# Splitting the mixers' weight chunks in one piece of 1024 columns instead of two of 512, all but the first

## The chip, the cores and the metric

The kernel runs on one core of a Trainium2 chip. The metric is the time of one execution on the device in microseconds (us): the median of the runs of the kernel before is 599.97 us (3 runs, 599.6 to 600.78). The profile is of one execution of its own.

## What is computed

The reference is a small decoder of two layers for 256 tokens of width 1024 in float32. Each layer has a mixer (self-attention and attention to a fixed memory, then an output projection) and an MLP with a squared ReLU of width 4096. Cut to what matters:

```python
# layer A
h = _rmsnorm(x, a_norm_attn);  z = h @ a_w_in          # q, k, v, qm
o_self = _diff_attention(rope(q), rope(k), v, lam, lam_init, a_subln)
o_mem = _memory_attention(qm, mem, a_mem_norm, a_w_mem_kv)
x = x + concat([o_self, o_mem]) @ a_w_out
x = x + relu(_rmsnorm(x, a_norm_mlp) @ a_w_up)**2 @ a_w_down
# layer B
k, v = _rmsnorm(x, kv_norm) @ w_kv;  z = _rmsnorm(x, b_norm_attn) @ b_w_in
o_self = _moba_attention(rope(q), rope(k), v)          # one block: causal attention
o_mem = _memory_attention(qm, mem, b_mem_norm, b_w_mem_kv)
x = x + concat([o_self, o_mem]) @ b_w_out
x = x + relu(_rmsnorm(x, b_norm_mlp) @ b_w_up)**2 @ b_w_down
return _rmsnorm(x, final_norm)
```

## The kernel before

**Weights.** All weights lie in DRAM as 192 chunks of 128 x 1024 float32 (512 KB each). `chunk()` (line 319) loads one into a buffer `w`, makes its high part `wh` with a cast on ACT (line 336) and its low part `wl` = w - wh with a subtraction on VectorE (DVE, line 338). Every matrix product then takes three matmuls on TensorE (PE): h·wh, h·wl, l·wh, where h and l are the high and low part of the activations. `split_scaled` (line 351) makes those, with one ACT instruction (L352) and one DVE instruction (L354) for a tile of 128 x 256.

The split of a chunk is done in two halves of 512 columns or in one piece, by `st_["pieces"]`. It starts at 2, `mlp_up` (line 778) sets it to 1 for a layer's MLP, and the end of `mlp` (line 996) sets it back to 2. So the 64 chunks of the two mixers are split in halves, those of the MLPs in one piece. A matmul that uses columns of one half waits for the split of that half alone.

**Stages.** A mixer has 24 chunks for its projections (`nat_block`, line 484, matmuls of 128 x 512 at L499; K tile k uses half k % 2 of chunk k // 2) and 8 for the output projection (`out_proj`, line 754). There, chunk after chunk, 8 blocks of three matmuls of 128 x 256 (L765) use one tile of 128 rows of the attention's output. The tiles are taken in the order of `OUT`: 4, 5, 6, 7, 0, 1, 2, 3. A tile comes from `finish_o` (line 628): two PE transposes of one pair of heads (L634), then L352 and L354. In layer A the attention's output is scaled before that: L721 (PE), L725 and L732 (ACT), a row of small DVE instructions ending with L399, and L744 on POOL. L586 (scores), L624 and L681 are other matmuls and transposes of the attention. The MLPs (L821 up, L871 down) follow each mixer.

**Order.** Every piece of work is a step of a planner (class `Plan`, line 59). Steps are added in program order; a step's priority is its number in that order, less a shift for its kind from the table `EARLY` (line 31), unless `pri` gives a number by hand; the lower goes first. `Plan.order` (line 118) plays the steps on the engines with a duration set for each, takes for a free engine the ready step of the best priority, and so fixes the order in which each engine's instructions are emitted. Each engine then runs its own in that order, one behind the other. Buffers are counted: 4 of class `w`, 6 of `wh`, 6 of `wl` (line 233). A chunk gets a buffer when a chunk before it has been used up, and `w`, `wh` and `wl` are given out in program order.

**The start.** A loop at the end of the kernel (lines 1274 to 1283) adds the loads of x in two parts (`xa` with the first four tiles of 256 tokens, `xb` with the last four, priority 3), the first four chunks, and the splits of x's eight tiles. The first chunk is loaded in two halves. Line 1282 sets by hand the priority of the step that stands fifth from the end of the list of steps, just after a chunk has been added: with one DMA step and four split steps that is the chunk's DMA. All loads are issued by SyncE (SP).

Of the kernel before, what the change touches and what calls it, by code (L numbers as in the profile page):

```python
# [208 lines left out]
def t_act(n, psum=False, scale=False):  # L209
    return (51 if psum else 93) + 0.835 * n + (93 if scale else 0)  # L210


def t_dve(n, scalar=False):
    return 69 + 1.041 * n + (61 if scalar else 0)
# [11 lines left out]
def tile_hybrid(ctx: ExitStack, tc: tile.TileContext, xa, xb, memt, xnat, mnat, w0, wall, consts, fgain, out):  # L226
# [17 lines left out]
    def buf(cls, shape, dt=F32, pool=None):  # L244
        pool = pool or ring
        return Buf(cls, lambda slot: pool.tile(shape, dt, name=name(cls), tag=f"{cls}{slot}", bufs=1))

    def bank(cls):
        return buf(cls, [128, 512], F32, psum)
# [62 lines left out]
    def dma(dst, src, nbytes, r=(), w=(), pri=None):  # L312
        P.add(("dma", max(470, nbytes / (290 if nbytes <= 2100 * 128 else 390)), lambda: nc.sync.dma_start(dst(), src)),
              r, w, lag=1900, pri=pri)


    st_ = {"i": 0, "pieces": 2, "layer": "A"}

    def chunk(dma_pieces=1):
        i = st_["i"]  # L320
        st_["i"] += 1
        w = buf("w", [128, CW])
        h = buf("wh", [128, CW], F32R)
        l = buf("wl", [128, CW], F32R)
        hs = (0, 1)
        if dma_pieces == 1:
            dma(lambda: w.t, wall[i], 4 * 128 * CW, w=[(w, 0), (w, 1)])
        else:
            for p in hs:
                dma(lambda p=p: w.t[:, p * 512:(p + 1) * 512], w0[p], 256 * CW, w=[(w, p)], pri=2 * p - 1.5)  # L330
        old, P.shift = P.shift, EARLY["w" + st_["layer"]]
        for p in (hs if st_["pieces"] == 2 else [hs]):
            q = p if isinstance(p, tuple) else (p,)
            sl = slice(q[0] * 512, q[-1] * 512 + 512)
            n = 512 * len(q)
            P.add(("act", t_act(n), lambda sl=sl: nc.scalar.copy(h.t[:, sl], w.t[:, sl])),  # L336
                  [(w, x) for x in q], [(h, x) for x in q])
            P.add(("dve", t_dve(n), lambda sl=sl: nc.vector.tensor_sub(l.t[:, sl], w.t[:, sl],  # L338
                                                                       h.t[:, sl].bitcast(F32))),
                  [(w, x) for x in q] + [(h, x) for x in q], [(l, x) for x in q], port=True)  # L340
        P.shift = old
        return h, l
# [8 lines left out]
    def split_scaled(src, skey, gain, T, k, psrc=False):  # L351
        P.add(("act", t_act(S, psrc, True), lambda: nc.scalar.activation(T.h(k), src(), AF.Copy, scale=gain)),  # L352
              skey, [T.hk(k)])
        P.add(("dve", t_dve(S, True), lambda: nc.vector.scalar_tensor_tensor(  # L354
            T.l(k), src(), gain, T.h(k).bitcast(F32), op0=OP.mult, op1=OP.subtract)),
            list(skey) + [T.hk(k)], [T.lk(k)], port=not psrc)
# [393 lines left out]
    def add_x(m, ps, off):  # L750
        P.add(("dve", t_dve(S), lambda: nc.vector.tensor_add(xT[:, m], xT[:, m], ps.t[:, off:off + S])),  # L751
              [ps, ("x", m)], [("x", m)])
# [59 lines left out]
    def ukeys(us, k):  # L812
        return [(us[k // 4], k // 2), (us[k // 4], k // 2, 1)]
# [21 lines left out]
    def block_sums():  # L835

        sums = {}
        for i, j in enumerate(FAST):
            if i < 2:
                b = ppx_buf()  # L840
                dst, keys = (lambda b=b: b.t), [b]
            elif i < 5:
                dst = lambda i=i: vb.rearrange("p a b e -> p (a b e)")[:, (i - 2) * 512:(i - 1) * 512]
                keys = [("vb", n, hf) for n in range(2) for hf in range(2)]
            else:
                dst, keys = (lambda: mv.rearrange("p a b e -> p (a b e)")), [("mv", 0), ("mv", 1)]
            sums[j] = dst, keys + [("s", j)]
        st_["sums"] = sums
        return sums
# [102 lines left out]
    def mlp(st, done):  # L952
        us = mlp_up(st, block_sums())
        pss = {(hf, c): bank("t") for c in range(2) for hf in range(2)}
        ys = {(hf, c): buf("q" + "hl"[c], [128, 512]) for hf, c in pss}

        def gather(more):
            r1, r5, r6, r7 = more

            def add(y, x, r):  # L960
                y, x = ys[y], ys[x]
                P.add(("dve", t_dve(512), lambda: nc.vector.tensor_add(y.t, x.t, r.t)), [x, r] + [y] * (x is y), [y])
            P.add(("act", t_act(512, True), lambda: nc.scalar.copy(ys[0, 0].t, r1.t)), [r1], [ys[0, 0]])
            add((0, 1), (0, 0), r6)
            add((1, 0), (0, 1), r7)
            add((1, 1), (1, 0), r5)
            add((0, 1), (0, 1), r5)

        part = 24
        _, product, u_ = natural_down(us, pss, part, part, gather,  # L970
                                      wsum, lambda a: [("wsum", a)], 4)
        for c in range(2):
            for k in range(part, 32):
                i = k % 2
                if i == 0:
                    ch = chunk()
                for hf in range(2):
                    product(pss[hf, c], u_(k, hf), lambda ch=ch, i=i: [b.t[:, i * 512:i * 512 + 512] for b in ch], 0, 512,
                            k == 31, ukeys(us, k) + [(b, i) for b in ch])
            for hf in range(2):  # L980
                y, ps = ys[hf, c], pss[hf, c]
                P.add(("dve", t_dve(512), lambda y=y, ps=ps: nc.vector.tensor_add(y.t, y.t, ps.t)), [y, ps], [y])
            for b in range(2):
                ps = bank("t")

                def turn(c=c, b=b, ps=ps):
                    for i in range(2):
                        for hf in range(2):
                            o = b * 256 + i * 128
                            nc.tensor.transpose(ps.t[:, i * S + hf * 128:i * S + hf * 128 + 128],  # L990
                                                ys[hf, c].t[:, o:o + 128], ident)
                P.add(("pe", 4 * 110 + 85, turn), [ys[0, c], ys[1, c]], [ps])
                for i in range(2):
                    add_x(4 * c + 2 * b + i, ps, i * S)
                    done(4 * c + 2 * b + i)
        st_["pieces"] = 2

    def mlp_last(st):

# [275 lines left out]
    for k in range(KT):  # L1275
        if k == 0:
            dma(lambda: xg[:, 0:NG + 4 * S], xa, 512 * (NG + 4 * S), w=["g"] + [("x", j) for j in range(4)], pri=-1)
        if k == 4:
            dma(lambda: xg[:, NG + 4 * S:], xb, 512 * 4 * S, w=[("x", j) for j in range(4, 8)], pri=3)
        if k % 2 == 0:  # L1280
            first_ch.append(chunk(2 if k == 0 else 1))
            P.steps[-5].pri = k - 0.5 if k else P.steps[-5].pri
        split_scaled(lambda k=k: xT[:, k], [("x", k), "g"], g["a_norm_attn"][:, k:k + 1], xn, k)
# [27 lines left out]
    rx = Stats()  # L1311
    xq = big_tiles(2, 3)
    mlp(ma, x_prep("kv_norm", xn, rx))

    def mem_b():
# [86 lines left out]
```

## Time and profile before

| | |
|---|---|
| median of 3 runs | 599.97 us (599.6 to 600.78) |
| span of the profiled execution | 725.8 us |
| mean granted TensorE clock in it | 0.755 |
| PE busy | 716.6 us, 99% of the span |
| DVE busy | 491.3 us, 68% |
| ACT busy | 398.0 us, 55% |
| DMA, mean rate | 149 GB/s |

The page gives no time of the profiled execution beside its span, which is 126 us longer than the median of the runs. How to read the lines that follow: a group is line, engine, operation, tile written <- tiles read, shape, then busy time in us, mean duration in ns, and after the second bar the idle time of the engine just ahead of these instructions with what ended it. A row of the timeline is start, length, engine, line, operation, tiles and count (neighbours of a kind stand in one row), with the idle time before it in brackets. A row of the chain of work that ended last is start, length, engine and line.

### The profile page before, as it was taken

How to read it: one execution, taken by the hardware profiler on the slowest of the kernel's cores; microseconds unless marked ns; L12 is line 12 of the kernel's file. 1: busy time of each engine (PE TensorE's matmuls, PEld its weight loads, DVE VectorE, ACT ScalarE, POOL GpSimd, SP SyncE). 2: the span in 40 equal slices, each digit the busy share in tenths (PEclk: the TensorE clock that was granted, in tenths of full speed). 3: DMA queues.
4: the chain of work that ended last, by engine and by line, in shares of the span. 5: the costliest groups of instructions: out<-in, count | busy, mean ns of one | idle time of the engine just before them, and what ended most of it. 6: DMA issues, size and time to landing. Idle time of an engine off the chain costs nothing.

```text
span 725.8 us, 10368 instructions
## 1 busy us (share of the span) xinstructions
PE 716.6 (99%) x3794; PEld 590.5 (81%) x3794; DVE 491.3 (68%) x871; ACT 398.0 (55%) x750; POOL 54.4 (8%) x67
## 2 busy tenths in 40 slices
PE   9999999999999999999999999999999999999996
PEld 7676769999999977677777776889999999776775
DVE  5777666587556687766776577675675666876664
ACT  6776666455544554444575477656464455554422
POOL 0121110030000000000111121001200000000002
PEclk8777777777777777777777777777777777777777
DMA  8854432435444433546455432224444443354421
GB/s 303 293 183 165 146 95 79 145 119 175 151 168 146 152 139 132 188 145 209 139 174 179 169 120 85 88 88 143 153 164 152 154 158 125 127 186 151 148 85 59
DMA packets 30003, 108.45 MB, mean 149 GB/s; under 512 B 3328, under 2 KB 3328, under 8 KB 29696
## 3 DMA queue, kind: packets, MB, share of 16 engines
q1 hardware_dynamic: 29664, 107.26, 43.4%
q8 instruction: 30, 0.49, 0.3%
q10 hardware_dynamic: 288, 0.52, 0.2%
q14 instruction: 21, 0.17, 0.1%
HBM read 106.72 MB, written 1.05 MB: 148 GB/s over the span
## 4 chain that ended last, share of the span: by engine, by line
PE 98%; DVE 1%; DMA 1%; ACT 0%; issue 0%; SPq 0%; ACTq 0%
PE acc L821 30%; PE acc L499 23%; PE t L871 23%; PE acc L765 7%; PE acc L871 6%; PE t L586 2%; PE t L624 2%; PE t L681 1%; PE t L557 1%; DMA xT<-xa 1%; PE t L1013 0%; PE t L990 0%; DVE xT L751 0%; PE t L579 0%; PE t L721 0%; PE t L720 0%
## 5 line engine op out<-in xcount | busy, mean ns | idle before, releaser
L336 ACT CAST wh<-w 128x512 fp32r<-128x512 f32 (+1 forms) x232 | 182.5, 814 | 191.3 <-PE acc L821 74.0
L338 DVE TENSOR_TENSOR wl<-w,wh 128x512 fp32r<-128x512 f32 (+1 forms) x232 | 213.4, 939 | 86.7 <-ACT wh L336 71.7
L821 PE MATMUL acc<-xn,wh 128*128 128x256 f32 x1024 | 157.3, 314 | 0.5 <-DVE xn L354 0.5
L821 PEld LDWEIGHTS acc<-xn,wh 128*128 128x128 f32 x1024 | 150.7, 224 | 0.7 <-DVE xn L354 0.7
L871 PE MATMUL t<-wh,B 128*128 128x512 f32 (+1 forms) x368 | 134.4, 453 | 0.0
L499 PE MATMUL acc<-wh,xn 128*128 128x512 f32 x256 | 101.6, 472 | 0.7 <-ACT xn L352 0.7
L871 PEld LDWEIGHTS t<-wh,B 128*128 128x128 f32 x368 | 72.5, 199 | 29.8
L821 PE MATMUL acc<-xn,wl 128*128 128x256 f32 x512 | 84.1, 314 | 0.0
L871 PE MATMUL t<-wl,B 128*128 128x512 f32 (+1 forms) x184 | 82.9, 450 | 0.0
L821 PEld LDWEIGHTS acc<-xn,wl 128*128 128x128 f32 x512 | 78.1, 224 | 0.0
L499 PEld LDWEIGHTS acc<-wh,xn 128*128 128x128 f32 x256 | 51.0, 199 | 23.5 <-issue 2.2
L765 PE MATMUL acc<-B,wh 128*128 128x256 f32 x256 | 60.1, 323 | 0.0
L499 PE MATMUL acc<-wl,xn 128*128 128x512 f32 x128 | 58.0, 453 | 0.0
L790 DVE SCALAR_TENSOR_TENSOR u<-acc,rb 128x512 f32<-128x512 f32 x32 | 21.9, 690 | 50.5 <-PE acc L821 50.5
L871 PEld LDWEIGHTS t<-wl,B 128*128 128x128 f32 x184 | 37.0, 201 | 15.1
L765 PEld LDWEIGHTS acc<-B,wh 128*128 128x128 f32 x256 | 46.3, 216 | 0.9 <-issue 0.8
L452 POOL TENSOR_TENSOR sqa<-sqa,sq 128x256 f32<-128x256 f32 x21 | 20.3, 966 | 295.7 <-ACT sq L451 294.9
L765 PE MATMUL acc<-B,wl 128*128 128x256 f32 x128 | 40.0, 313 | 0.0
L895 DVE TENSOR_TENSOR wl<-wsum,wh 128x1024 fp32r<-128x1024 f32 x24 | 29.4, 1223 | 8.9 <-ACT wh L894 6.5
L533 POOL TENSOR_TENSOR ropet<-ropes,consts 128x256 f32<-128x256 f32 (+1 forms) x28 | 25.1, 917 | 129.0 <-ACT ropes L522 106.5
L499 PEld LDWEIGHTS acc<-wl,xn 128*128 128x128 f32 x128 | 26.8, 210 | 9.1
L894 ACT CAST wh<-wsum 128x1024 fp32r<-128x1024 f32 x24 | 25.3, 1052 | 15.9 <-PE acc L871 6.9
(223 smaller groups left out, 899.1 us busy)
## 6 DMA issues: line engine op xcount, KB each, us to landing
w<-wall SPq DMA_DIRECT2D x191, 512.0 KB, 3.3
w<-memt SPq DMA_DIRECT2D x4, 512.0 KB, 5.0
B<-xnat SPq DMA_DIRECT2D x1, 1024.0 KB, 7.4
B<-mnat SPq DMA_DIRECT2D x1, 1024.0 KB, 8.9
xT<-xa SPq DMA_DIRECT2D x1, 540.0 KB, 3.8
w<-w SPq DMA_DIRECT2D x2, 256.0 KB, 3.5
xT<-xb SPq DMA_DIRECT2D x1, 512.0 KB, 6.6
consts<-consts SPq DMA_DIRECT2D x1, 256.5 KB, 4.5
```

What stands on the lines that cost most here:

```text
L336: P.add(("act", t_act(n), lambda sl=sl: nc.scalar.copy(h.t[:, sl], w.t[:, sl])), [(w, x) for x in q], [(h, x) for x in q])
L338: P.add(("dve", t_dve(n), lambda sl=sl: nc.vector.tensor_sub(l.t[:, sl], w.t[:, sl], h.t[:, sl].bitcast(F32))), [(w, x) for x in q] + [(h, ...
L452: P.add(("pool", t_pool(S), lambda: nc.gpsimd.tensor_tensor(self.acc.t, self.acc.t, sq.t, op=OP.add)), [sq, self.acc], [self.acc])
L499: nc.tensor.matmul(pss[hf].t[:, c0:c1], a(k)[:, ts], b.t[:, o + c0:o + c1], start=(k == 0 and i == 0), stop=(k == KT - 1 and i == 2))
L533: nc.gpsimd.tensor_tensor(t.t[:, 0:nh, e:e + 32], zs.t[:, 0:nh, 32 - e:64 - e], b(sin[:, e:e + 32]), op=OP.mult)
L586: nc.tensor.matmul(sp[hd].t[:, c], qk[a].t[r, qb * 128:(qb + 1) * 128], qk[b].t[r, S:S + c.stop - c.start], start=(qb == 0 and i == 0 and ...
L765: nc.tensor.matmul(o, a.t[:, ws], x(k), start=(n == 0 and m % 2 == 0 and i == 0), stop=(n == KT - 1 and i == 2), skip_group_check=True)
L790: P.add(("dve", t_dve(512, True), lambda u=u, ps=ps: nc.vector.scalar_tensor_tensor(u.t, ps.t.rearrange("p (a s) -> p a s", a=2), 0.0, rb_ ...
L821: nc.tensor.matmul(ps.t[:, o], w.t[:, k * 128:(k + 1) * 128], xnt[:, k, x], skip_group_check=True, **flags)
L871: nc.tensor.matmul(ps.t[:, c0:c1], x, y, start=start and i == 0, stop=stop and i == 2, skip_group_check=True)
L894: P.add(("act", t_act(m), lambda: nc.scalar.copy(h[x].t[:, :m], src())), keys, [h[x]])
L895: P.add(("dve", t_dve(m), lambda: nc.vector.tensor_sub(l[x].t[:, :m], src(), h[x].t[:, :m].bitcast(F32))), keys + [h[x]], [l[x]], port=True)
```

## The change

`mlp` no longer sets `st_["pieces"]` back to 2, and the loop of the start sets it to 2 for the first chunk and to 1 for the others. With that, 63 of the 64 mixer chunks are split by one ACT and one DVE instruction of 128 x 1024.

```diff
@@ mlp
                 for i in range(2):
                     add_x(4 * c + 2 * b + i, ps, i * S)
                     done(4 * c + 2 * b + i)
-        st_["pieces"] = 2
@@ the start
         if k % 2 == 0:
+            st_["pieces"] = 2 if k == 0 else 1
             first_ch.append(chunk(2 if k == 0 else 1))
             P.steps[-5].pri = k - 0.5 if k else P.steps[-5].pri
```

A chunk that is split in one piece adds three steps to the planner's list, not five. The step that is fifth from the end in line 1282 is then no longer the chunk's DMA, but a split step of a tile of x that was added before it; the DMAs of chunks 1, 2 and 3 keep the priority of their place in the list. And as every mixer chunk adds two steps fewer, the numbers from which priorities are made are others, so that the planner puts the steps of both mixers in another order, on all engines. The order of the MLPs is nearly the same.

At the start of SP's queue (w_224 is the first chunk, w_230 or w_234 the second, xT<-xa and xT<-xb the halves of x; - is before, + is after):

```order
 L313 DMA xT_66<-xa 128x1080
 L313 DMA w_224<-w 128x512
-L313 DMA w_230<-wall 128x1024
 L313 DMA xT_66<-xb 128x1024
-L313 DMA w_246<-wall 128x1024
-L313 DMA w_261<-wall 128x1024
+L313 DMA w_234<-wall 128x1024
+L313 DMA w_242<-wall 128x1024
+L313 DMA w_257<-wall 128x1024
 L313 DMA consts_68<-consts 128x513
```

The second half of x has moved ahead of the second chunk. At the same place on ACT (xn are the split tiles of x, w_230 and w_234 the second chunk):

```order
 L352 ACTIVATE xn_67<-xT_66 128x256 x3
 L336 CAST wh_228<-w_224 128x512
-L352 ACTIVATE xn_67<-xT_66 128x256
-L336 CAST wh_254<-w_230 128x512 x2
+L352 ACTIVATE xn_67<-xT_66 128x256 x5
+L336 CAST wh_270<-w_234 128x1024
```

All splits of x's tiles now stand ahead of the second chunk's cast. At the end of layer A's mixer, on ACT before (t_1484 and t_1505 are the transposes of the last two pairs of heads, B_275_1058 the high parts of the attention's output):

```order
L725 ACTIVATE o_1420<-t_1405,rs_175 128x128 x2
L732 ACTIVATE dg_1431,msq_180<-o_1420 128x128 x2
L336 CAST wh_1466<-w_1223 128x1024
L352 ACTIVATE B_275_1058<-t_1484,consts_68 128x256
L336 CAST wh_1503<-w_1304 128x1024
L352 ACTIVATE B_275_1058<-t_1505,consts_68 128x256
```

and in the changed kernel (t_1462 and t_1468 are the same two transposes, wh_1434 and wh_1457 chunks of the MLP):

```order
L725 ACTIVATE o_1402<-t_1392,rs_175 128x128 x2
L732 ACTIVATE dg_1413,msq_180<-o_1402 128x128 x2
L336 CAST wh_1434<-w_1198 128x1024
L336 CAST wh_1457<-w_1271 128x1024
L352 ACTIVATE B_276_1014<-t_1462,consts_68 128x256
L352 ACTIVATE B_276_1014<-t_1468,consts_68 128x256
```

Both casts now stand ahead of both L352; on DVE the subtractions of the same chunks stand ahead of both L354 likewise. On PE at the same place, in the changed kernel (wh_1128 is chunk 5 and wh_1169 chunk 6 of the output projection, acc are its sums):

```order
L765 MATMUL acc_1157<-B_276_1014,wh_1128 128x256
L765 MATMUL acc_1157<-B_276_1014,wl_1145 128x256
L765 MATMUL acc_1157<-B_278_1021,wh_1128 128x256
L634 MATMUL t_1462<-ident_122,o_1330 128x128 x2
L634 MATMUL t_1468<-ident_122,o_1402 128x128 x2
L765 MATMUL acc_1130<-B_276_1014,wh_1169 128x256
L765 MATMUL acc_1130<-B_276_1014,wl_1183 128x256
L765 MATMUL acc_1130<-B_278_1021,wh_1169 128x256
```

The transposes of both pairs stand between chunk 5's last matmul and chunk 6's first. Before, 30 matmuls of chunks 4 and 5 stood between the first of them and chunk 6, and 18 between the second and chunk 6.

## The prediction

> **What bounds the kernel now.** I read the page first: the span, the busy shares, the granted clock and the shares of the chain of work that ended last.
>
> ```profile
> span 725.8 us, 10368 instructions
> PE 716.6 (99%) x3794; PEld 590.5 (81%) x3794; DVE 491.3 (68%) x871; ACT 398.0 (55%) x750; POOL 54.4 (8%) x67
> PEclk8777777777777777777777777777777777777777
> PE 98%; DVE 1%; DMA 1%; ACT 0%; issue 0%; SPq 0%; ACTq 0%
> core 0: 725.8 us, clock 0.755
> ```
>
> The last row is from the view of the cores. In this execution TensorE (PE) is busy for 716.6 of 725.8 us and the chain is PE for 98%. Two engines feed it: ACT makes the high part of each weight chunk, VectorE (DVE) the low part. They have 45% and 32% of idle time, so shorter splits by themselves buy nothing here. But the granted clock is 0.755, and the span stands 126 us above the median of the runs, 599.97. The timed runs therefore had another balance, which bounds as follows. PE work at full clock would be about 716.6 x 0.75 = 537 us. With the 9 us in which PE is not busy that makes 546, so the 600 leave some 54 us for waits if the clock was full; without any further wait, 600 - 9 = 591 us for the same work means a clock of 537 / 591 = 0.91. The truth lies between: a clock of 0.91 and no waits, or full clock and 54 us of waits for ACT, DVE or DMA. I look for where such waits would be, in the windows by stage (columns: window, its length, busy time of PE, PEld, DVE, ACT and POOL with counts, granted clock, DMA share, GB/s).
>
> ```profile
> 10.00:50.00 40.00, 40.00 (x161) 28.06 (x159) 28.47 (x61) 28.12 (x65) 6.49 (x6) 0.75 0.76 267
> 50.00:100.00 50.00, 50.00 (x226) 35.83 (x223) 37.39 (x94) 35.90 (x109) 6.92 (x8) 0.75 0.41 133
> 100.00:150.00 50.00, 49.51 (x327) 44.17 (x326) 31.76 (x77) 31.79 (x84) 3.85 (x6) 0.75 0.33 108
> 400.00:450.00 50.00, 50.00 (x234) 35.16 (x233) 32.49 (x66) 31.68 (x79) 10.34 (x12) 0.75 0.36 119
> 450.00:500.00 50.00, 50.00 (x349) 43.19 (x348) 30.77 (x73) 27.85 (x71) 0.00 (x0) 0.75 0.30 99
> ```
>
> At full clock PE would need 30 us for the first row and 37.5 for the second; DVE is busy for 28.5 and 37.4 there. So layer A's mixer is where DVE would bind in a faster run, and the mixers are what the change touches.
>
> **What the larger pieces save.** The groups with their shapes kept apart:
>
> ```profile
> L338 DVE TENSOR_TENSOR wl<-w,wh 128x1024 fp32r<-128x1024 f32 x104 | 127.7, 1229 | 51.0 <-ACT wh L336 37.0 <-PE acc L821 9.8 <-PE acc L871 2.1
> L336 ACT CAST wh<-w 128x1024 fp32r<-128x1024 f32 x104 | 109.1, 1051 | 151.5 <-PE acc L821 74.0 <-PE t L871 61.3 <-PE acc L765 14.7
> L338 DVE TENSOR_TENSOR wl<-w,wh 128x512 fp32r<-128x512 f32 x128 | 85.8, 704 | 35.6 <-ACT wh L336 34.7 <-issue 0.8
> L336 ACT CAST wh<-w 128x512 fp32r<-128x512 f32 x128 | 73.4, 621 | 39.8 <-PE acc L499 24.6 <-PE t L871 5.7 <-DMA w<-wall 3.6
> ```
>
> 128 halves are the 64 mixer chunks. 63 of them become one piece: 63 instructions fewer on ACT and 63 on DVE. Twice a mean is too much, since neighbours overlap: two halves in a row take 1.14 us on ACT and 1.29 on DVE (rows below), so a chunk saves about 0.09 on ACT and 0.06 on DVE, together 63 x 0.09 = 5.7 us and 63 x 0.06 = 3.8 us. In the profiled execution this is beside a busy PE: worth 0. In a timed run it is worth at most the 3.8 us of the tighter engine. I take 0.5 us: of the three rows of layer A's mixer only the middle one has DVE at what PE would need, so about a third of that mixer's half of 3.8, which is 0.6.
>
> [...]
>
> **The start (term 1).** Fewer steps per chunk move the hand-set priority in line 1282 from the chunk's DMA to another step, so on SP the second half of x goes ahead of chunk 1 (the order is shown above). ACT follows suit: all of x is split ahead of chunk 1. The timeline of the start, and two rows of the page's table of DMAs:
>
> ```profile
> 2.11 0.43 SPq L313 DMA_DIRECT2D w<-wall  x1
> 2.59 0.43 SPq L313 DMA_DIRECT2D xT<-xb  x1
> 8.00 1.14 ACT L336 CAST wh<-w 128x512 fp32r<-128x512 f32 x2 [0.77 <-DMA w<-wall]
> 8.65 1.29 DVE L338 TENSOR_TENSOR wl<-w,wh 128x512 fp32r<-128x512 f32 x2 [0.72 <-ACT wh L336]
> 9.26 1.71 ACT L352 ACTIVATE xn<-xT 128x256 fp32r<-128x256 f32 x4
> 10.83 0.47 PE L499 MATMUL acc<-wl,xn 128*128 128x512 f32 x1
> w<-wall SPq DMA_DIRECT2D x191, 512.0 KB, 3.3
> xT<-xb SPq DMA_DIRECT2D x1, 512.0 KB, 6.6
> ```
>
> Chunk 1 is issued at 2.11, and ACT waits for it until 8.00; x's second half, issued at 2.59, lands 6.6 us later, at 9.2. The two transfers are of 512 KB each, so I let them change places: x at 8.0, the chunk at 9.2. Then ACT's four splits of x last until 8.0 + 1.71 = 9.71, the cast of the whole chunk until 9.71 + 1.05 = 10.76, and DVE's subtraction until 10.76 + 0.04 + 1.23 = 12.03. PE wants the low part of chunk 1 at 10.83, in its row: this is its fifth matmul on a low part, and the four before it, two for each of two K tiles, use chunk 0. It waits 1.2 us, with a hop 1.25. Bounds: 0, if the wait is made up behind it; and 1.95, if the chunk lands another 1.2 us later, at 10.4, 0.7 after ACT is free for it. For the making up speak these rows on chunks 4 and 5:
>
> ```profile
> 17.81 1.13 ACT L336 CAST wh<-w 128x512 fp32r<-128x512 f32 x2
> 20.48 1.15 ACT L336 CAST wh<-w 128x512 fp32r<-128x512 f32 x2 [1.54 <-DMA w<-wall]
> ```
>
> The second cast waits for its DMA. In the profiled execution PE runs on without a gap until after them, so the 1.25 stays. A faster PE would come to wait for those transfers and take back a part; I take 1.0 for a timed run.
>
> **The end of layer A's mixer (term 2).** The output projection has 24 matmuls per chunk. Its chunks 6 and 7 need the last two heads' outputs turned and split: PE transposes (L634), ACT's L352, DVE's L354. The rows:
>
> ```profile
> 119.50 3.41 PE acc L765 x24
> 125.46 0.31 PE t L634 x2
> 134.81 0.46 PE L634 MATMUL t<-ident,o 128*128 128x128 f32 x2
> 135.31 0.48 ACT L352 ACTIVATE B<-t,consts 128x256 fp32r<-128x256 f32 x1 [1.81 <-PE t L634]
> 135.82 0.48 DVE L354 SCALAR_TENSOR_TENSOR B<-t,consts,B 128x256 fp32r<-128x256 f32 x1 [0.91 <-ACT B L352]
> 136.16 1.05 ACT L336 CAST wh<-w 128x1024 fp32r<-128x1024 f32 x1 [0.37 <-PE acc L765]
> 137.25 1.23 DVE L338 TENSOR_TENSOR wl<-w,wh 128x1024 fp32r<-128x1024 f32 x1 [0.94 <-ACT wh L336]
> 138.39 0.48 DVE L354 SCALAR_TENSOR_TENSOR B<-t,consts,B 128x256 fp32r<-128x256 f32 x1
> ```
>
> The first two are from the chain: 3.41 / 24 = 0.142 us a matmul, 0.31 for a pair of transposes. Before, the transposes of the first of these heads stand 30 matmuls ahead of their use and those of the second 42, and PE does not wait. In the changed order both pairs stand directly ahead of chunk 6. On ACT two casts, and on DVE their two subtractions, stand ahead of the splits. The second cast takes the sixth and last buffer of its class, the one that chunk 5 holds; so it starts only after chunk 5's last matmul, which stands directly ahead of the transposes. From that matmul's start: it ends at 0.31, the cast runs from 0.35 to 1.40, the subtraction from 1.44 to 2.67, the split L354 of the first head from about 2.6 to 3.06, and the matmul on its low part can start at 3.1. PE, without a wait, is there after one matmul, two pairs of transposes and two matmuls: 0.142 + 0.62 + 0.284 = 1.05. **The wait is 2.05 us**; I take 2.1. Behind the waiting matmul on PE's queue stand all of chunks 6 and 7, the last residual adds and the MLP, so nothing fills it. The second head's L354 ends at about 3.55, and its use stands 24 x 0.142 = 3.4 us behind the first's: no wait there. Bounds: 0, if the cast gets its buffer sooner than I count; 3.1, if nothing of the chain lies beside PE. At full clock PE's 1.05 shrink to 0.8 and the wait becomes 2.3.
>
> **The rest.** In layer B's mixer the same splits get longer, but the order leaves at least 10 matmuls of L765 behind the last attention products, 10 x 0.142 = 1.4 us, as cover for the ACT and DVE splits of 0.48 each; I cost it at 0. If that cover were gone, its price would be that of term 2. The MLPs keep their order: 0.
>
> **The sum.** On the profiled execution: 725.8 + 1.25 + 2.05 = 729.1 us, 0.45% more. On the median of the runs: 599.97 + 1.0 + 2.3 - 0.5 = **602.8 us**.
>
> **Rivals.** Slower or faster is told from the measurement by over 0.2%, 1.2 us.
>
> (a) Faster, because DVE is the bound in the mixers. If the timed clock is above about 0.95, PE's need in the second window is 37.5 / 0.95 = 39.5 us or less against DVE's 37.4 in its dependent chain, and every 0.06 us saved on DVE comes through; the waits of terms 1 and 2 then fall into time in which PE waited already. 599.97 - 3.8 + 1.0 for the part of the start that stays = 597.2. For it: the 54 us of waits if the clock was full, and DVE's 37.39. Against it: the profile's clock is 0.755, and the only wait on PE's chain is 1% DVE. Chance 0.22.
>
> [...]
>
> (b) No change. Layer A's half of DVE's savings comes through, 31 x 0.06 = 1.9 us, the start's wait is taken back at chunks 4 and 5, and term 2 stays: 599.97 + 2.1 - 1.9 = 600.2. Chance 0.23.
>
> (c) Slower still. A short step that is queued behind a split can now wait 1.05 instead of 0.62 us on ACT and 1.23 instead of 0.70 on DVE, 0.96 along a chain of both. If two of the attention's chains in the mixers have PE waiting, as a faster clock would make them, 602.8 + 1.9 = 604.7. For it: the five rows of windows, with ACT and DVE each at over 27 of 50 us. Against it: no such wait in the profile before. Chance 0.15.
>
> (d) The change doesn't do what its words say at the start: if the two transfers run side by side and land together, their order matters little, term 1 is 0 and the time is 601.8. It belongs to the forecast's side.
>
> **How the numbers follow.** The forecast with (d) has 0.40, (a) 0.22, (b) 0.23, (c) 0.15. Of the forecast's 0.40 all lies above 601.2, of (b) nearly all within 598.8 to 601.2: slower 0.55, same 0.23, faster 0.22. The range of 8 in 10 takes in (b), (c) and the milder half of (a): from 598.0 up to (c) with the upper bound of the start, 604.7 + 1.4 = 606.1. The forecast's own range is 601.2 to 604.
>
> **What would show it.** After: 128x1024 casts x167 and 128x512 x2 (as the counts 104 + 63 say). At the start, a wait of PE L499 for the low part of chunk 1, ended by DVE L338 near 12 us, of about 1.2 us: term 1. Ahead of chunk 6 of L765, a wait of about 2 us ended by DVE L354, with a cast and a subtraction of 128x1024 just before on ACT and DVE: term 2. If PE shows neither gap, the order did not bite. If the span rises by 3 us but the timed median falls, the savings on DVE decide in the timed runs: rival (a). Waits at L624 or L586 in the mixers would speak for (c).

## The result and the profile after

The changed kernel takes 605.99 us (median of 4 runs, 604.42 to 609.76), the kernel before on the same chip 599.79: a ratio of 1.0128, with a 95% interval of 1.0086 to 1.0171. Run again on another chip it was 603.59 against 597.92, 1.0108 (1.0087 to 1.0130). So the change costs 1.1 to 1.3% by the ratios, 5.7 to 6.2 us by the medians. The forecast had the direction, and 2.8 us, less than half of that; 605.99 lies at the upper end of its wide range (598.0 to 606.1) and above its own (601.2 to 604).

The page of the changed kernel, and its row in the view of the cores:

```profile
span 603.8 us, 10239 instructions
PE 586.4 (97%) x3794; PEld 515.9 (85%) x3794; DVE 480.6 (80%) x811; ACT 382.6 (63%) x684; POOL 56.6 (9%) x67
PE 77%; DVE 2%; ACT 0%; issue 0%; DVEq 0%; ACTq 0%
core 0: 603.8 us, clock 0.998
```

This execution had a clock of 0.998, not 0.755. It can't be laid beside the profile that the forecast was made from, so the first experiment was to profile the kernel before again. It too got 0.998:

```profile
span 595.2 us, 10368 instructions
PE 583.7 (98%) x3794; PEld 514.5 (86%) x3794; DVE 485.5 (82%) x871; ACT 390.4 (66%) x750; POOL 56.1 (9%) x67
```

That answers the first question of the forecast: the four timed runs of the changed kernel were granted a clock of 0.994 to 0.998. The two profiles differ by 8.6 us. DVE and ACT have 4.9 and 7.8 us less to do after, somewhat more than the 3.8 and 5.7 that the forecast had for the saved instructions, and the kernel is slower all the same. Where the time goes is read from the first matmul of each stage in the timeline: L821 opens an MLP, and the first L990 stands at the same place near the end of layer A's MLP. Before:

```profile
125.28 0.86 PE L821 MATMUL acc<-xn,wh 128*128 128x256 f32 x6
288.60 1.03 PE L990 MATMUL t<-ident,qh 128*128 128x128 f32 x8
414.47 0.75 PE L821 MATMUL acc<-xn,wh 128*128 128x256 f32 x5
```

After:

```profile
129.12 0.75 PE L821 MATMUL acc<-xn,wh 128*128 128x256 f32 x5
292.44 1.03 PE L990 MATMUL t<-ident,qh 128*128 128x128 f32 x8
419.67 0.52 PE L821 MATMUL acc<-xn,wh 128*128 128x256 f32 x3
```

Layer A's mixer takes 3.8 us longer, its MLP the same 163.3, layer B's mixer 127.2 instead of 125.9. Those are the two mixers, 5.2 us together. Another 3.0 us lie in layer B's MLP, 176.5 from its start to the start of PE's last matmul instead of 173.5, though its order is nearly the same; they are taken up at the end. The remaining 0.4 us stand behind PE's last matmul. This pair of profiles overstates layer A's mixer, as the next section shows.

### The profile page after: what moved, and what is told of

The parts are those of the page before. It is cut to its first block, busy times and chain, and to the rows that moved or that the text cites. A ratio compares the mean times of both kernels' runs of the same rounds, so it can differ in the third digit from the quotient of the medians.

```text
span 603.8 us, 10239 instructions
## 1 busy us (share of the span) xinstructions
PE 586.4 (97%) x3794; PEld 515.9 (85%) x3794; DVE 480.6 (80%) x811; ACT 382.6 (63%) x684; POOL 56.6 (9%) x67
## 3 DMA queue, kind: packets, MB, share of 16 engines
HBM read 106.72 MB, written 1.05 MB: 178 GB/s over the span
## 4 chain that ended last, share of the span: by engine, by line
PE 77%; DVE 2%; ACT 0%; issue 0%; DVEq 0%; ACTq 0%
PE acc L821 29%; PE t L871 22%; PE acc L499 11%; PE acc L871 6%; PE acc L765 5%; PE t L586 1%; PE t L624 1%; PE t L681 1%; PE t L557 1%; DVE wl L338 1%; DVE xT L751 0%; PE t L990 0%; PE t L1012 0%; DVE xn L354 0%; ACT wh L336 0%
## 5 line engine op out<-in xcount | busy, mean ns | idle before, releaser
L336 ACT CAST wh<-w 128x1024 fp32r<-128x1024 f32 (+1 forms) x169 | 175.4, 1047 | 133.2 <-PE acc L821 44.5
L338 DVE TENSOR_TENSOR wl<-w,wh 128x1024 fp32r<-128x1024 f32 (+1 forms) x169 | 206.5, 1229 | 39.5 <-ACT wh L336 38.7
L821 PE MATMUL acc<-xn,wh 128*128 128x256 f32 x1024 | 130.2, 279 | 1.1 <-DVE xn L354 1.1
L821 PEld LDWEIGHTS acc<-xn,wh 128*128 128x128 f32 x1024 | 123.4, 188 | 1.5 <-DVE xn L354 1.3
L871 PE MATMUL t<-wh,B 128*128 128x512 f32 (+1 forms) x368 | 111.9, 386 | 0.0
L499 PE MATMUL acc<-wh,xn 128*128 128x512 f32 x256 | 85.3, 401 | 2.7 <-ACT xn L352 1.5
L821 PE MATMUL acc<-xn,wl 128*128 128x256 f32 x512 | 70.1, 279 | 0.0
L821 PEld LDWEIGHTS acc<-xn,wl 128*128 128x128 f32 x512 | 64.0, 188 | 0.0
L452 POOL TENSOR_TENSOR sqa<-sqa,sq 128x256 f32<-128x256 f32 x21 | 20.1, 955 | 238.2 <-ACT sq L451 237.2
L605 ACT ACTIVATE B<-t,nm 128x128 f32<-128x128 f32 (+1 forms) x64 | 27.1, 449 | 9.0 <-DVE nm L601 7.1
L793 ACT ACTIVATE u<-u 128x512 f32<-128x512 f32 x32 | 20.1, 632 | 16.3 <-DVE u L790 16.2
```

Of the source, the lines that this page charges most:

```text
L452: P.add(("pool", t_pool(S), lambda: nc.gpsimd.tensor_tensor(self.acc.t, self.acc.t, sq.t, op=OP.add)), [sq, self.acc], [self.acc])
L499: nc.tensor.matmul(pss[hf].t[:, c0:c1], a(k)[:, ts], b.t[:, o + c0:o + c1], start=(k == 0 and i == 0), stop=(k == KT - 1 and i == 2))
L605: nc.scalar.activation(p[hd].t[:, c], sp[hd].t[:, c], AF.Exp, bias=nm[hd][:, qb:qb + 1], accum_out=ss[:, hd, qb:qb + 1])
L793: P.add(("act", t_act(512), lambda u=u: nc.scalar.activation(u.t, u.t, AF.Square)), [u], [u])
L821: nc.tensor.matmul(ps.t[:, o], w.t[:, k * 128:(k + 1) * 128], xnt[:, k, x], skip_group_check=True, **flags)
L871: nc.tensor.matmul(ps.t[:, c0:c1], x, y, start=start and i == 0, stop=stop and i == 2, skip_group_check=True)
```

## The experiments

Every profile below has a clock of 0.99 or more. Ratios are to the kernel before on the same chip; "mixer A" is the time to the first L821, "mixer B" that from the first L990 to the L821 of the second layer, read as above.

| run | median us, before | ratio (95% interval) | mixer A | mixer B |
|---|---|---|---|---|
| before again | 597.45, 597.06 | 1.0005 (0.9994 to 1.0015) | 125.3 | 125.9 |
| before's order, whole pieces | 599.23, 597.06 | 1.0040 (1.0024 to 1.0056) | 126.2 | 126.3 |
| changed order, halves | 604.07, 597.06 | 1.0106 (1.0091 to 1.0122) | 130.3 | 127.6 |
| DMA priority mended | 603.50, 597.06 | 1.0103 (1.0089 to 1.0117) | 129.9 | 127.2 |
| changed kernel again | 603.59, 597.92 | 1.0108 (1.0087 to 1.0130) | 128.7 | 127.3 |
| change in mixer A alone | 600.76, 597.92 | 1.0060 (1.0041 to 1.0078) | 129.1 | 125.9 |
| change in mixer B alone | 598.93, 597.92 | 1.0018 (1.0002 to 1.0035) | 127.9 | 127.3 |
| tail mended | 600.85, 597.92 | 1.0060 (1.0041 to 1.0079) | 127.2 | 127.3 |
| tail and a place in B mended | 601.90, 598.18 | 1.0050 (1.0031 to 1.0068) | 127.4 | 127.7 |
| before, one subtraction moved | 598.80, 598.18 | 0.9999 (0.9972 to 1.0026) | 127.2 | 125.9 |
| start in halves | 603.90, 598.18 | 1.0084 (1.0048 to 1.0121) | 129.8 | 127.3 |
| all mended | 605.46, 598.18 | 1.0101 (1.0061 to 1.0141) | 129.8 | 127.7 |
| before, whole pieces in A | 598.83, 597.58 | 1.0017 (0.9993 to 1.0041) | 126.3 | 125.8 |
| before, whole pieces in B | 598.08, 597.58 | 1.0005 (0.9981 to 1.0029) | 126.2 | 126.3 |
| before, x first | 597.41, 597.58 | 0.9999 (0.9976 to 1.0021) | 125.9 | 125.8 |
| mixer A alone, tail mended | 599.51, 597.58 | 1.0027 (1.0004 to 1.0050) | 127.1 | 125.9 |

Mixer A of one profile is uncertain by about 1.3 us: the same order and halves there gave 125.3, 126.2, 127.2 and 127.9, on average 126.7. The changed mixer A gave 128.7, 129.1 and 129.1, on average 129.0. By these averages the change costs 2.3 us there, not the 3.8 of the first pair.

**Order or length of the pieces.** The change does two things, so the four combinations were laid side by side. Before's order with whole pieces (the place of the first half does all, that of the second nothing):

```diff
+            if st_["pieces"] == 2 and i:
+                sl = slice(0, 512 * (1 - p) * 2)
-            P.add(("act", t_act(n), lambda sl=sl: nc.scalar.copy(h.t[:, sl], w.t[:, sl])),
+            P.add(("act", t_act(n), lambda sl=sl: sl.stop and nc.scalar.copy(h.t[:, sl], w.t[:, sl])),
...
```

The changed order with halves:

```diff
+            mix = n == CW and (i < 32 or 96 <= i < 128)
+            sls = [slice(0, 512), slice(512, CW)] if mix else [sl]
-            P.add(("act", t_act(n), lambda sl=sl: nc.scalar.copy(h.t[:, sl], w.t[:, sl])),
+            P.add(("act", t_act(n), lambda sls=sls: [nc.scalar.copy(h.t[:, sl], w.t[:, sl]) for sl in sls]),
...
```

> The kernel before, unchanged, to have its profile at the clock that the timed runs have (the changed kernel's was granted 0.998, that of before 0.755). Theory: span near 598 us, PE idle about 6 us less than the 17.4 us of the changed kernel, the gaps of the changed kernel at 9.5 to 12 us and at 120.7 to 123.5 us not there. Rival (longer pieces keep PE waiting everywhere a little): idle less by small amounts in all mixer windows, no single gap gone.

> The order of before on every engine, with the 63 mixer chunks split in one piece at the place of the first half (the second half's place stays empty). Theory that the order costs the time: 598 to 600.5 us, like before. Rival that the longer pieces cost it: 604 to 606 us, like the changed kernel. Rival that the saved instructions gain: 596 to 597 us.

> The order of the changed kernel on every engine, with each of the 63 splits emitted as two halves one behind the other. Theory that the order costs the time: 605 to 608 us. Rival that the longer pieces cost it: 599 to 601 us.

Measured: 1.0040 and 1.0106. With the order of the changed kernel the halves are no faster than the whole pieces (1.0106 against 1.0108). So the loss is that of the order. The whole pieces cost a little instead of saving at before's order, and at the changed order they make no difference that could be measured. Where they can cost is seen in the waits of PE. In the kernel before (columns: who waits, for whom, us in all, times, the longest):

```profile
PE acc L499 <- ACT wh L336: 1.1, 1, 1.1
PE acc L499 <- DVE wl L338: 0.2, 1, 0.2
```

and at before's order with whole pieces (its lines are two higher):

```profile
PE acc L501 <- DVE wl L340: 2.4, 4, 0.8
PE acc L501 <- ACT wh L338: 0.9, 2, 0.5
```

The first projections use each chunk as it lands. PE now waits four times for the low part of a chunk, up to 0.8 us, because the whole subtraction has to end where the first half would have done. That these waits are the 0.40% is not shown. PE's waits at this line for both parts of the chunks come to 3.3 us here and 3.5 in the other profile of this order with whole pieces in layer A, and to 1.3, 1.9, 2.6 and 4.1 in the four profiles of halves; mixer A is 126.2 and 126.3 against 125.3 to 127.9. Two later runs did this in one mixer only, with the condition `0 < i < 32` or `i > 32` in place of `i`:

> The order of before, with whole pieces in layer A's mixer alone (at the place of the first half). The same in both mixers was 1.0040. Theory (whole pieces cost where chunks are used as they land, in layer A's projections): 1.002 to 1.004. Rival (the forecast's saving of 0.06 us of DVE a chunk comes through): 0.998 to 1.000.

> The order of before, with whole pieces in layer B's mixer alone. From the profile with both: 0.5 us more than before in this mixer, 1.0005 to 1.0015. Rival (all of the 1.0040 is here): 1.003 to 1.004.

1.0017 and 1.0005. The best estimates put it in layer A, but both intervals hold 1. Only the loss with whole pieces in both mixers, 1.0040, is clear of the noise.

**The first transfers.** First the changed kernel with the priority back on the DMA:

```diff
-            P.steps[-5].pri = k - 0.5 if k else P.steps[-5].pri
+            P.steps[-3].pri = k - 0.5 if k else P.steps[-3].pri
```

> The changed kernel with the hand-set priority on the chunks' DMA again, so that chunk 1 is loaded ahead of the second half of x; PE's order is that of the changed kernel. By term 1 of the forecast: 1.0 to 1.3 us less than the changed kernel, about 604.7 us. Rival that later waits for transfers take it back: 605.5 to 606.3 us, no gain.

1.0103 against 1.0108: 0.3 us by the estimates, not the 1.0 to 1.3 of term 1; the two ran on different chips, and their intervals hold 1.0 us as well. The same from the other side is the kernel before, its order kept but for the second half of x loaded and split ahead of chunk 1:

```diff
+    for what, ahead in [("xb", ("load", 1))] + [((e, k), (c, 1, 0)) for k in range(4, 8)
+                                                for e, c in (("xh", "cast"), ("xl", "sub"))]:
+        if plan.index(at[what]) > plan.index(at[ahead]):
+            plan.remove(at[what])
+            plan.insert(plan.index(at[ahead]), at[what])
```

> The kernel before with halves, its order kept but for the start: the second half of x is loaded and split ahead of chunk 1, as in the changed kernel. Term 1 without the longer piece: chunk 1 lands 1.2 us later, so 0.6 to 1.2 us slower, 1.001 to 1.002. Rival (PE waits for later transfers anyway and takes it back): 0.9995 to 1.0005.

0.9999 (0.9976 to 1.0021). The step is in the profile as forecast, but it costs nothing that could be measured; a loss of 1.0 us, 1.0017, is still inside the interval. The timeline of the changed kernel's start:

```profile
7.95 1.71 ACT L352 ACTIVATE xn<-xT 128x256 fp32r<-128x256 f32 x4 [0.23 <-DMA xT<-xb]
9.56 2.03 ACT L336 CAST wh<-w 128x1024 fp32r<-128x1024 f32 x2
10.62 2.36 DVE L338 TENSOR_TENSOR wl<-w,wh 128x1024 fp32r<-128x1024 f32 x2 [0.45 <-ACT wh L336]
10.65 0.50 PE L499 MATMUL acc<-wh,xn 128*128 128x512 f32 x1 [1.13 <-ACT wh L336]
11.90 0.50 PE L499 MATMUL acc<-wl,xn 128*128 128x512 f32 x1 [0.76 <-DVE wl L338]
```

x lands at 7.95 (forecast 8.0), and the low part of chunk 1 is used at 11.90 (12.03). PE waits there for 1.13 and 0.76 us, more than the forecast's 1.25. In the kernel before it waits later instead, for a cast that stands on ACT behind six splits L352, which had waited for the load of the memory:

```profile
27.61 2.51 ACT L352 ACTIVATE wh<-w,xT 128x256 fp32r<-128x256 f32 x6 [0.38 <-DMA w<-memt]
30.39 1.13 ACT L336 CAST wh<-w 128x512 fp32r<-128x512 f32 x2
31.05 0.51 PE L499 MATMUL acc<-wh,wh 128*128 128x512 f32 x1 [1.09 <-ACT wh L336]
```

A last run on the start kept the changed order, with the priority mended, and split chunks 1 to 7 alone in halves (`i < 8` as the condition):

> The changed kernel with its order kept, the hand-set DMA priority mended, and the splits of chunks 1 to 7 alone emitted as two halves. Theory (at the start, where chunks are used as they land, a longer piece delays the first use by about 0.97 us: 1.05 - 0.62 on ACT and 1.23 - 0.69 on DVE): 0.7 to 1.2 us less than the changed kernel with the priority mended, 1.0085 to 1.009. Rival (the transfers bound the start): 1.0105 as there.

1.0084, with an interval from 1.0048 to 1.0121: it can't tell 1.0085 from 1.0105. Inconclusive.

**Which mixer.** Whole pieces (and so the new order) in one mixer only; the diff is line 996 kept for A, and removed without the new line for B.

> The changed kernel again, beside before on one chip. In its first profile 3.0 us of its loss lay in layer B's MLP, whose order is the same and which takes 173.5 us in every other profile here. If that was the chip: 1.009 to 1.011 times before. If it belongs to the kernel: 1.013 again.

> Whole pieces in layer A's mixer alone, so that the order of layer A is that of the changed kernel and the order of layer B's mixer that of before. Theory (start 1.0 to 1.5, end of the mixer 2.3 to 2.8): 3.8 to 4.6 us slower than before. Rival that the loss lies in layer B's mixer and MLP: 0 to 2 us slower.

> Whole pieces in layer B's mixer alone; layer A's order is that of before. Theory: 1.2 to 1.5 us slower than before (two waits of PE on ACT L510 and DVE L565). The forecast's own term for this mixer: 0. Rival: 3 to 4 us, with layer B's MLP slower too.

1.0060 and 1.0018, that is 3.6 and 1.1 us, each a little less than expected and with the expected values inside its interval. They add up to 0.78%, and the changed kernel has 1.08% (from 0.87): what is missing is within the intervals. In layer B's mixer it is the order again: with the changed order and halves it takes 127.6 us, no less than with whole pieces (127.2 to 127.3).

**The end of layer A's mixer.** The timeline of the changed kernel there, from the last subtractions of the chain to PE's first matmul on the split output:

```profile
119.70 1.23 DVE L338 TENSOR_TENSOR wl<-w,wh 128x1024 fp32r<-128x1024 f32 x1
119.96 2.02 POOL L744 TENSOR_TENSOR o<-o,rr 128x256 f32<-128x256 f32 x2 [9.80 <-DVE rr L399]
120.38 0.28 PE L765 MATMUL acc<-B,wh 128*128 128x256 f32 x1
120.69 1.04 ACT L336 CAST wh<-w 128x1024 fp32r<-128x1024 f32 x1 [1.83 <-PE acc L765]
121.46 1.01 PE L634 MATMUL t<-ident,o 128*128 128x128 f32 x4 [0.80 <-POOL o L744]
121.77 1.28 DVE L338 TENSOR_TENSOR wl<-w,wh 128x1024 fp32r<-128x1024 f32 x1 [0.84 <-ACT wh L336]
121.93 1.05 ACT L352 ACTIVATE B<-t,consts 128x256 fp32r<-128x256 f32 x2 [0.19 <-PE t L634]
122.98 0.86 DVE L354 SCALAR_TENSOR_TENSOR B<-t,consts,B 128x256 fp32r<-128x256 f32 x2
123.50 0.50 PE L765 MATMUL acc<-B,wh 128*128 128x256 f32 x2 [0.54 <-DVE B L354]
```

The chain of term 2 is there step by step: cast, subtraction, L354, and PE waits for it. From the start of chunk 5's last matmul (120.38) to the first matmul on the low part (123.50) 3.1 us pass, as forecast. One link was not forecast: PE waits 0.80 us for POOL already at the transposes. L744 lies beside the subtraction of 119.70, and its two instructions take 2.02 us instead of the 1.18 or 1.19 of the other two places in this profile. (They take 2.17 us at this place in the kernel before too; there the transposes come later and PE does not wait.) The mending moves one cast and two subtractions of later chunks behind the splits, PE's order kept:

```diff
+    for move, behind in ((("cast", 35), ("Ah", 3)), (("sub", 34), ("Al", 3)), (("sub", 35), ("sub", 34))):
+        plan.remove(at[move])
+        plan.insert(plan.index(at[behind]) + 1, at[move])
```

("cast" and "sub" are a chunk's split steps, "Ah" and "Al" the L352 and L354 of the last pair of heads.)

> The changed kernel, with one cast and two subtractions of the MLP's first chunks moved behind the splits L352 and L354 of the last two pairs of heads, on ACT and DVE; PE's order is kept. Theory (these three stand in the chain, and the subtraction beside POOL's L744 lengthens it): 1.0 to 1.6 us less than the changed kernel, L744 at 1.2 instead of 2.0 us, PE's wait for DVE L354 at 0.5 us or less. Rival (the transposes simply stand too near to their use): 0 to 0.4 us less.

1.0060 against 1.0108: 2.7 us by the medians, 2.9 by the ratios. The rows that answer to those above (lines one to three higher):

```profile
119.41 1.18 POOL L747 TENSOR_TENSOR o<-o,rr 128x256 f32<-128x256 f32 x2 [9.79 <-DVE rr L401]
119.84 0.28 PE L768 MATMUL acc<-B,wh 128*128 128x256 f32 x1
120.08 1.01 PE L636 MATMUL t<-ident,o 128*128 128x128 f32 x4
120.56 1.04 ACT L354 ACTIVATE B<-t,consts 128x256 fp32r<-128x256 f32 x2 [2.23 <-PE t L636]
121.06 1.06 DVE L356 SCALAR_TENSOR_TENSOR B<-t,consts,B 128x256 fp32r<-128x256 f32 x2 [1.82 <-ACT B L354]
121.60 0.51 PE L768 MATMUL acc<-B,wh 128*128 128x256 f32 x2
122.03 2.35 DVE L339 TENSOR_TENSOR wl<-w,wh 128x1024 fp32r<-128x1024 f32 x2
```

POOL is back at 1.18, the wait for it is gone, and L354 starts 0.5 us behind L352 instead of a subtraction later. From chunk 5's last matmul (119.84) to the first on the low part (121.60) 1.8 us pass instead of 3.1: the profiles give 1.3 to 1.4 us for the mending. The same with the change in mixer A alone:

> Whole pieces and the new order in layer A's mixer alone (1.0060), with its end mended. If the end and the rest of that mixer are all: 1.3 us of the end's 2.4 are mended, so 1.0035 to 1.0045. If the end is worth more than its profile shows (the changed kernel gained 2.9 us by the mending): 1.001 to 1.002.

1.0027 against 1.0060: 2.0 us by the ratios. The gains of 2.0 and 2.9 us have intervals of some 1.7 us either way, so they can't be told from the 1.3 that the profiles show. 1.6 us of layer A's loss stay. About 1.0 of it is at this end, as the transposes still stand directly ahead of their use: 1.8 us pass there, where PE's own work is 0.8 by the forecast's estimate. No run shows what the rest is.

**Layer B's mixer.** A wait of PE in the timeline of the changed kernel:

```profile
382.09 1.04 ACT L336 CAST wh<-w 128x1024 fp32r<-128x1024 f32 x1
383.23 1.22 DVE L338 TENSOR_TENSOR wl<-w,wh 128x1024 fp32r<-128x1024 f32 x1
383.39 0.60 ACT L564 CAST qh<-t 128x512 fp32r<-128x512 f32 x1
384.37 0.68 DVE L565 TENSOR_TENSOR ql<-t,qh 128x512 fp32r<-128x512 f32 x1
385.11 0.33 PE L586 MATMUL t<-qh 64*128 64x128 f32 x2 [0.44 <-DVE ql L565]
```

A cast and a subtraction stand ahead of the two short steps that PE waits for. They were moved behind them, on top of the mended tail (`move(("cast", 125), ("qh", nxt))` and the like for the subtraction):

> The changed kernel with the end of layer A's mixer mended as in the run on the tail, and in layer B's mixer the one cast and one subtraction that stand ahead of L564 and L565 at 382 us moved behind them; PE's order is kept. Theory (a long piece ahead of a short step that PE waits for): 0.3 to 0.7 us less than with the tail mended alone, so 1.004 to 1.0055 times before, and no wait of PE for DVE L565. Rival (the order of PE itself costs it): 1.006 as with the tail alone.

The wait for L565 is gone, and another has come in its place (PE's transposes L557, two lines higher here, on a DVE instruction that the subtraction now stands ahead of):

```profile
384.78 1.10 PE L559 MATMUL t<-ident,B 128*128 128x128 f32 x8 [0.86 <-DVE B L689]
```

Mixer B takes 127.7 us, no less than without this mending; the 1.0050 can't be told from 1.0060. Its loss is measured, 1.1 us by the run with that mixer alone and 1.3 to 1.4 by the profiles, but no mending gave it back, so its cause is not shown.

**A version to beat both.** Both kernels wait 1.1 us at the start of layer A's MLP for L354, with a subtraction of an MLP chunk ahead of it on DVE. In the kernel before, that one was moved behind the splits (`move(("sub", 36), ("a_norm_mlp", 7))`).

> The kernel before (halves in the mixers) with one subtraction of an MLP chunk moved on DVE from ahead of the five splits L354 of the normed x to behind them, at the start of layer A's MLP; nothing else. Both kernels have PE wait 1.1 us there for L354. Theory (the subtraction of 1.2 us in that chain is the wait): 0.8 to 1.1 us faster than before, 0.998 to 0.9985 times it. Rival (PE then waits for the moved subtraction, or for L751): no gain.

0.9999, with an interval that holds the expected 0.998 too. In the profile the wait went, and PE waited 0.9 us for POOL's L452 instead (three lines higher here), 10 us later; layer A's MLP took 163.5 us, as against 163.3:

```profile
138.21 0.61 PE L463 MATMUL t<-ones,sqa 128*128 128x1 f32 x4 [0.89 <-POOL sqa L455]
```

And all of it in the changed kernel:

> All of it in the changed kernel: priority mended, chunks 1 to 7 in halves, the tail, layer B's place, and the subtraction at the start of layer A's MLP moved. If the named places are the whole loss and add up: 1.000 to 1.002 times before. If something else costs as much again: 1.004 or more.

1.0101. The mendings don't add up. The moved subtraction brought that same wait for POOL, but this is not why layer A's MLP took 166.2 us instead of 163.3: with the same wait it took 163.5 in the run before. The view of waits lists no other wait of PE in that MLP in either run: it is a step of 3 us like the one taken up at the end. Nor is it known whether the other executions of this run had it. Mixer A took 129.8 us, and from its second pair of L744 to L821 it took the 18.8 us of the mended end (20.1 without), so the loss lies ahead of that. No version was found that beats the kernel before. The table `EARLY`, whose shifts count steps, was left as it is; whether other shifts give whole pieces a better order was not tried.

## Why the forecast was right in sign and wrong in size

- **The step that failed** is the price of the new order away from the two places that were worked out, together with the gain set against them. The order alone costs 1.06%, 6.3 us; the forecast had 1.0 + 2.3 for the start and the end of layer A's mixer, 0 for layer B's mixer, and took 0.5 off for larger pieces. The runs show 1.1 us in layer B's mixer and no gain that could be measured from larger pieces at either order. What else the order costs stays open.
- **The clock** was taken as unknown between 0.91 and 1; it was 0.99 and more. What followed for term 2 (2.3 at full clock) was right to use. The "54 us of waits" at full clock, on which rival (a) leaned, were wrong: PE's whole busy time was scaled by 0.75 to 537 us, but at a clock of 0.998 PE is busy for 583.7 us of 595.2. In layer B's MLP, matmuls of 128 x 256 took 0.140 us each at a clock of 0.75 (20 us / 143, from 540 to 560 us) and 0.113 at 1.00 (50 us / 443), a factor of 0.81.
- **Term 2, the end of layer A's mixer**, 2.3 us: the chain held, with 3.1 us from chunk 5's last matmul to the first on the low part. Less the 0.8 of PE's own work this is the 2.3. The sign named for it, a wait of about 2 us ended by L354, did not come: PE waits 0.80 us for POOL, whose two L744 took 2.02 us beside the subtraction and 1.18 with it moved away, and 0.54 for L354. The wait for POOL was not in the forecast; it falls into the time that the cast and subtraction take anyway. The mending gave back 1.3 us in the profiles.
- **Term 1, the start**, 1.0 us: failed by the best estimates (0.3 and 0 us), though the intervals still hold 1.0. x and the low part of chunk 1 came when worked out, to 0.2 us, and PE's waits were longer than the 1.25. But the lower bound, "0, if the wait is made up behind it", is nearer to what was measured: with x first, layer A's first L586 starts at 43.3 us, and in the four profiles of halves in before's order at 42.9 to 45.8. The chain of the kernel before passes through two loads behind the start (start, length, what):

```profile
14.51 7.04 DMA w<-wall
27.12 5.42 DMA w<-wall
```

- **"I take 0.5 us" for what the larger pieces save**: failed, with the wrong sign at before's order. There they cost 0.40%, 2.4 us (1.0 and 0.3 by the estimates for each mixer alone); at the changed order they cost nothing that could be measured. ACT and DVE had less to do, as forecast, but the pieces were weighed by throughput alone. That the time to the first half counts where a chunk is used as it lands is the likely reason; it is argued from PE's waits, not shown.
- **"I cost it at 0", layer B's mixer**: failed. It is 1.1 us by the run with that mixer alone, 1.3 to 1.4 by the profiles. The cover of 10 matmuls was counted at its end, where PE has no wait; the waits lie in its middle, at L557 and L586, of which the forecast named L586 only as a sign of rival (c). The one at L586 is a short step behind a chunk's split, as (c) has it. But both come with halves in the changed order as well (0.4 and 0.5 us), so they come with the order, not with the longer piece that (c) had in mind. That (c) was the nearest case in time, with 1.9 us for two such chains, is in part luck.
- **Rivals (a) and (b)** fell. The clock was over 0.95, the point from which (a) was to decide, and DVE's saved time still didn't reach PE. (d) had term 1 at 0 for another reason than the one found: the transfers did change places, and x landed first.
- **The upper end of the range**, 606.1, adds 1.4 us to (c) for the start. By the forecast's own numbers it is 1.95 - 1.0 = 0.95, which gives 605.7, a little under the 605.99 measured first.

With the runs' sizes the sum is 3.6 us in layer A (2.3 at its end, 1.3 that no run accounts for) and 1.1 in layer B, or 4.7, and the changed kernel has 6.5 by its ratio on the second chip (5.2 to 7.8 by its interval). What the remainder is stays open; the 3.0 us below are one candidate, as they come in some runs and not in others.

## What to carry to other kernels

A chunk split in halves took 0.06 us more on DVE and 0.09 more on ACT here than one in one piece (1.29 against 1.23, 1.14 against 1.05), and its first half was done after 0.70 and 0.62 us; where work is used as it arrives, or where a short step may stand behind it, count the wait, not the busy time. When a change alters how many steps a list scheduler sees, treat the new order as the change: keep the old order with the new pieces, and the new order with the old, before reasoning about either. A wait that is removed by moving one instruction can come back further on in the queues, as it did twice here.

## What the runs showed of the hardware

**A step of 3.0 us in layer B's MLP.** It takes 173.5 us in all but two of the 17 profiles at a clock of 0.99 or more. In the first one of the changed kernel it was 176.5, and in that of the kernel before with x first as well, two kernels with the same work there. The view of windows shows no wait of PE in them, the same clock as in the kernel before, and fewer matmuls in 50 us. The kernel before:

```profile
430.00:480.00 50.00, 50.00 (x443) 50.00 (x442) 40.81 (x64) 31.44 (x41) 0.00 (x0) 1.00 0.59 200
```

With x first:

```profile
430.00:480.00 50.00, 50.00 (x427) 50.00 (x426) 39.57 (x62) 30.18 (x39) 0.00 (x0) 1.00 0.57 191
```

PE and its weight loads are both busy throughout, at 0.113 us a matmul (50 / 443) in the one and 0.117 in the other. The first profile of the changed kernel has 429 matmuls there; from 450 to 480 us it has 257, and the run with the DMA priority mended 267, that is 0.117 us a matmul (30 / 257) against 0.112 (30 / 267). The step of 2.9 us in layer A's MLP with all mended has no listed wait of PE beside the 0.9 us for POOL. The cause was not tried. So 3.0 of the 8.6 us between the two first profiles are not the change's.

**POOL beside DVE.** In the changed kernel two L744 took 1.18 us beside reductions on DVE (L601), and 2.02 beside a subtraction of 128x1024; with the subtraction moved away they took 1.18 at that place. In the kernel before they took 2.17 there at a clock of 0.998, and 1.19 in the profile at 0.755, with DVE idle for the first 0.9 us of them. So the price of POOL work in a chain depended here on what DVE ran at that moment.

**A clock of 0.755 in one execution.** Of 18 profiles one, that of the kernel before from which the forecast was made, was granted 0.75 from 10 us on, and its span was 725.8 us. PE waited less in it: without the 1.1 us at L287, it waits there for ACT and DVE for 1.2 us in all, and for 3.1 us in the same kernel at 0.998. A shorter dip came too: from 0 to 24 us the mean clock was 0.93 in the second profile of the changed kernel, and 1.00 in its first.
